# Level-four scores computed in one piece with levels 16, 32, 64 and the key transposes

## The chip, the cores and the metric

The kernel runs on one core of one Trainium2 chip. The metric is the device time of one execution in microseconds, the median over the runs of a kernel. The core has a matrix engine (PE, with its weight loads shown as PEld), a vector engine (DVE), a scalar engine (ACT), GpSimd (POOL) and a sync engine (SP) that mostly issues DMAs. Each engine works through its own queue in order and waits on semaphores for the others.

## What is computed

One layer of a decoder trunk on a sequence of 1024 tokens of width 1024, all in float32: an RMS norm modulated by a conditioning vector, one input projection, two recurrent mixers side by side, a gated merge of both, an output projection and a final norm. The two mixers are HGRN2 with 8 heads (key and value width 128) and GLA with 4 heads (key width 128, value width 256). Both run the same chunked gated linear attention; of the reference this is the part that matters here:

```python
def step(S, inp):
    qi, ki, vi, gi = inp
    b = jnp.cumsum(gi, axis=2)
    o_inter = jnp.einsum('bhck,bhkv->bhcv', qi * jnp.exp(b), S)
    diff = b[:, :, :, None, :] - b[:, :, None, :, :]
    decay = jnp.where(causal, jnp.exp(jnp.minimum(diff, 0.0)), 0.0)
    scores = jnp.einsum('bhtk,bhsk,bhtsk->bhts', qi, ki, decay)
    o_intra = jnp.einsum('bhts,bhsv->bhtv', scores, vi)
    b_last = b[:, :, -1:, :]
    S_new = S * jnp.exp(b_last[:, :, 0, :])[..., None] + jnp.einsum(
        'bhsk,bhsv->bhkv', ki * jnp.exp(b_last - b), vi)
    return S_new, o_inter + o_intra
```

## The kernel before

The projections are long matmuls: a feature block (`Feat`, L454) is 48 matmuls of 128x128 weights with 512 columns, each operand split into a rounded part and a remainder; blocks of values (`Vblk`, `Vblk2`) are built alike. They stand in a list of jobs. While a job is emitted, every unit of some six long matmuls calls `weave`, which advances a second track, `side`: the attention of one head after another, written as a generator. Each `yield n` in it asks for n units at a pace of 1.1 before the generator goes on, so the yields set how many long matmuls lie between two pieces of a head. A third track, `back`, does background work (`factors`, `weight_sums`, `gate_side`). After the jobs come the last stages (L1313), again with `weave`; the twelfth head runs there. Behind all that a planner gives each engine its final order, from what it thinks will be ready when, so a later instruction can pass an earlier one that it takes to be waiting.

`attention` works on one head, keys and queries as tiles of 128 partitions (the key channel) by 1024 tokens, in chunks of 128. The decay between two tokens is a product of per-channel gates, so scores are built from the small to the large: within groups of four tokens (matmuls L596, 32 of 80 columns), then between the four members of groups of sixteen tokens, the level of four (L628, 32 of 48 columns), then between neighbouring blocks of 16 (L683, 32 of 16 columns), of 32 (L689, 16) and of 64 tokens (L694, 8). All write the one PSUM tile `sc_ps` of two banks. Between the levels DVE multiplies the gates into the queries and keys in place (L612, L630, L633; `grow` for the levels 16, 32, 64, L656 to L659), and before each `grow` of levels 16 and 32 ACT copies the halves that the matmuls of that level need out of q and k into parts of the tile `xb` (`keep`, L648). Level 64 reads q and k themselves. Masked copies on DVE (L603 to L611 for the first level, L669 to L672 for the level of four, L698 for level 16) collect the small scores in `blk`; ACT copies (L703 to L709) put everything into `scT`. Then the keys are transposed on PE (L720, 7 transposes through PSUM tiles of the pool `ps_m`) and copied out by ACT (L721) into `kT`; state products (L742) and their accumulation (L746, L748 on DVE) and the outputs (L761, L763) follow.

The order of a head's pieces on PE, with the yields between them, is: L596, 5, L628, 7, levels 16 to 64, 3.5, transposes, 1.5, state products, 3 and so on. A set `scoring` holds a head until its scores have left `sc_ps`; the last stages ask it before they lend `sc_ps` out as an accumulator.

SBUF tiles of 4 KB per partition come from `Slots`, 46 of them, handed out first in, first out. `Stream.ahead` loads the weights of a job two jobs ahead and splits them one job ahead, if enough slots are free; `factors` and `weight_sums` wait until 12 are.

Of the kernel before, what the change touches and what calls it, by code (L numbers as in the profile page):

```python
# [15 lines left out]
P = 128  # L16
D = 1024
T = 1024
KT = D // P
NCH = T // P  # L20
# [62 lines left out]
def hybrid_trunk_kernel(  # L83
# [6 lines left out]
    nc = tc.nc  # L90
# [9 lines left out]
    S = Slots(sp, N_SLOTS)  # L100
# [7 lines left out]
    def mtile():  # L108
        cnt[0] += 1
        return ps_m.tile([P, 512], F32, tag="m", name=f"pm{cnt[0]}")  # L110

    sc_ps = ps_s.tile([P, T], F32, name="sc_ps")


    ident = cp.tile([P, P], F32, name="ident")
# [214 lines left out]
    for bi, (d0, nd) in enumerate(blocks):  # L330
        if bi:
            make_mod(d0, nd, mods.pop(bi), 0)
        for d in range(d0, d0 + nd):
# [12 lines left out]
            for f in range(NG):  # L346
                for n, (a, b) in enumerate(((0, h_hi), (1, h_hi), (0, h_lo))):
                    nc.tensor.matmul(accs[f], wg(a, d, f), b[d][:, 0:512],
                                     start=(d == 0 and n == 0), stop=(d == KT - 1 and n == 2))
# [220 lines left out]
    def attention(q, k, f, v, vo, V, post):  # L570
# [23 lines left out]
        for b in range(32):  # L594
            ch, j = b // 4, b % 4
            nc.tensor.matmul(sc_ps[32 * j:32 * j + 32, ch * P:ch * P + 80], k[:, b * 32:b * 32 + 32], xb[:, b, :],  # L596
                             start=True, stop=True)
# [27 lines left out]
        yield 5  # L625
        for b in range(32):
            ch, j = b // 4, b % 4
            nc.tensor.matmul(sc_ps[32 * j:32 * j + 32, ch * 48:ch * 48 + 48], k[:, b * 32:b * 32 + 32],  # L628
                             xf[:, b * 48:b * 48 + 48], start=True, stop=True)
# [11 lines left out]
        kept = {}  # L641
        off = [320, tot[:, 256:320]]

        def keep(n):
            at = 0 if n == 16 else 1024
            kept[n] = flat[:, at:at + 512], flat[:, at + 512:at + 1024]
            for dst, src in zip(kept[n], (pairs(k, n)[:, :, 0, :], pairs(q, n)[:, :, 1, :])):
                nc.scalar.copy(dst.rearrange("p (b n) -> p b n", n=n), src)  # L648
# [13 lines left out]
        keep(16)  # L662
# [10 lines left out]
        grow(16)  # L673
        keep(32)
        grow(32)
        yield 7


        k16, q16 = kept[16]
        k32, q32 = kept[32]  # L680
        for b in range(32):
            ch, j = b // 4, b % 4
            nc.tensor.matmul(sc_ps[32 * j:32 * j + 16, 512 + ch * 16:512 + ch * 16 + 16],  # L683
                             k16[:, b * 16:b * 16 + 16], q16[:, b * 16:b * 16 + 16], start=True, stop=True)
        for ch in range(NCH):
            for hf in range(2):
                i = 2 * ch + hf
                p0, c0 = 64 * hf + 32 * (ch % 2), ch // 2 * 32
                nc.tensor.matmul(sc_ps[p0:p0 + 32, c0:c0 + 32], k32[:, i * 32:i * 32 + 32],  # L689
                                 q32[:, i * 32:i * 32 + 32], start=True, stop=True)  # L690
        for ch in range(NCH):
            s0 = ch * P
            p0, c0 = ch % 2 * 64, 640 + ch // 2 * 64
            nc.tensor.matmul(sc_ps[p0:p0 + 64, c0:c0 + 64], k[:, s0:s0 + 64],  # L694
                             q[:, s0 + 64:s0 + 128], start=True, stop=True)
        grow(64)
        cur = off[1]
        cpr(blk[:, :, 16:32], bc(masks[16], [NCH, 16]),  # L698
            sc_ps[:, 512:640].rearrange("p (c t) -> p c t", c=NCH))
        for hf in range(2):  # L700
            for odd in range(2):
                p0 = 64 * hf + 32 * odd
                nc.scalar.copy(scT[64 * hf:64 * hf + 32, odd::2, 64 * hf + 32:64 * hf + 64],  # L703
                               sc_ps[p0:p0 + 32, 0:128].rearrange("p (c t) -> p c t", t=32))
# [6 lines left out]
        yield 3.5  # L711


        kT = S.get([NCH, P])
        for g in range(2):
            nt = 4 if g == 0 else 3
            pt = mtile()
            for i in range(nt):
                ch = g * 4 + i
                nc.tensor.transpose(pt[:, i * P:(i + 1) * P], k[:, ch * P:(ch + 1) * P], ident)  # L720
            nc.scalar.copy(kT[:, g * 4:g * 4 + nt, :].rearrange("p c s -> p (c s)"), pt[:, 0:nt * P])  # L721
        S.free(k)
        yield 1.5
# [817 lines left out]
```

## Time and profile before

| | |
|---|---|
| median of 3 runs | 1249.74 us (1246.07 to 1254.04) |
| the profiled execution | 1252.38 us, span of its profile 1250.7 us |
| mean granted clock of PE | 0.99 |
| busy: PE, PEld | 1205.7 us (96%), 999.9 us (80%) |
| busy: DVE, ACT, POOL | 765.2 us (61%), 530.4 us (42%), 132.4 us (11%) |

A row of a profile names a line of the kernel, the engine, the operation, the tiles written and read, shapes, a count and durations; where a fence is from the timeline, it begins with start and duration in us. PE's busy time counts overlapping matmuls once, and a matmul's duration reaches beyond the start of the next, so the pace of PE is read from the starts. A wait is put down to the semaphore that came last. The profiled execution is one of several, so its own time is not the median.

### The profile page before, as it was taken

What the parts mean: (1) busy time and instruction counts of PE and PEld (TensorE: products, weight loads), DVE (VectorE), ACT (ScalarE), POOL (GpSimd) and SP (SyncE); (2) the same over time, 40 slices, a digit from 0 to 9 for tenths busy, and PEclk for the clock granted to TensorE, in tenths of its full rate; (3) what the DMA queues carried; (4) which work ended last, traced back from release to release, by engine and by line L of the source; (5) the groups of instructions that cost most, each with busy time, mean ns of one, the idle gap of its engine ahead of it and who ended that gap; (6) DMA issues with size and microseconds to landing.
All of it is one profiled execution on the core that took longest, in us unless ns stands there. A gap on an engine that the chain in (4) does not pass through costs nothing.

```text
span 1250.7 us, 20782 instructions
## 1 busy us (share of the span) xinstructions
PE 1205.7 (96%) x8603; PEld 999.9 (80%) x8603; DVE 765.2 (61%) x1219; ACT 530.4 (42%) x784; POOL 132.4 (11%) x216
## 2 busy tenths in 40 slices
PE   4799999999999999999999999999999999998997
PEld 3676899989798888788887878877888888787786
DVE  5746425494857556777873365695422668979443
ACT  4467713343334344243332323456643644454222
POOL 5510000201211021021110101011110000000000
PEclk9899999999999999999999999999999999999999
DMA  8832100653644167255251212154546556235202
GB/s 269 278 115 86 52 18 18 217 188 102 203 143 144 63 208 254 92 179 174 96 177 45 60 41 68 38 183 169 173 163 225 179 171 201 83 100 170 118 34 101
DMA packets 126928, 168.82 MB, mean 135 GB/s; under 512 B 7019, under 2 KB 97185, under 8 KB 126834
## 3 DMA queue, kind: packets, MB, share of 16 engines
q1 hardware_dynamic: 115234, 129.53, 33.5%
q0 software_dynamic: 11552, 37.97, 7.8%
q8 instruction: 67, 1.10, 0.4%
q14 instruction: 27, 0.22, 0.1%
q10 hardware_dynamic: 48, 0.01, 0.0%
HBM read 125.53 MB, written 41.94 MB: 134 GB/s over the span
## 4 chain that ended last, share of the span: by engine, by line
PE 59%; issue 24%; DVE 8%; DMA 3%; POOL 2%; ACT 2%; SPq 1%; POOLq 0%; DVEq 0%; ACTq 0%
PE pd L454 13%; PE pd L1313 11%; PE sc_ps L1313 5%; PE pm L1313 5%; PE pd L556 2%; PE pd L557 2%; PE pd L558 2%; DVE scT L250 1%; PE pm L761 1%; PE pm L742 1%; PE pm L763 1%; PE pd L1083 1%; PE pd L1084 1%; PE pd L1085 1%; DVE b L195 1%
## 5 line engine op out<-in xcount | busy, mean ns | idle before, releaser
L454 PE MATMUL pd<-b,b 128*128 128x512 f32 x1632 | 386.3, 393 | 0.0
L454 PEld LDWEIGHTS pd<-b,b 128*128 128x128 f32 x1632 | 302.4, 188 | 64.0 <-issue 0.5
L1313 PE MATMUL pd<-b,b 128*128 128x512 f32 x720 | 175.7, 395 | 2.5 <-DVE b L866 1.5
L1313 PEld LDWEIGHTS pd<-b,b 128*128 128x128 f32 x720 | 134.7, 189 | 35.4 <-DVE b L866 1.9
L195 DVE TENSOR_TENSOR b<-b,b 128x1024 fp32r<-128x1024 f32 (+1 forms) x95 | 101.8, 1082 | 74.7 <-ACT b L192 34.8
L192 ACT CAST b<-b 128x1024 fp32r<-128x1024 f32 (+1 forms) x95 | 84.6, 904 | 104.0 <-DVE b L1169 14.7
L1256 DVE TENSOR_TENSOR b<-b,b 128x1024 fp32r<-128x1024 f32 x56 | 68.3, 1224 | 68.5 <-ACT b L1255 46.6
L1255 ACT CAST b<-b 128x1024 fp32r<-128x1024 f32 x56 | 58.5, 1051 | 62.8 <-PE pd L1313 17.2
L1313 PE MATMUL sc_ps<-b,b 128*128 128x512 f32 x324 | 79.0, 391 | 0.3 <-ACT scT L706 0.3
L1313 PE MATMUL pm<-b,b 128*128 128x512 f32 x300 | 72.5, 389 | 3.4 <-DVE b L1256 3.4
L513 PE MATMUL pd<-b,b 128*128 128x256 f32 x256 | 74.2, 290 | 0.0
L515 PE MATMUL pd<-b,b 128*128 128x256 f32 x256 | 72.5, 283 | 0.0
L514 PE MATMUL pd<-b,b 128*128 128x256 f32 x256 | 72.4, 283 | 0.0
L1313 PEld LDWEIGHTS sc_ps<-b,b 128*128 128x128 f32 x324 | 60.4, 188 | 13.6 <-ACT scT L706 0.8
L1313 PEld LDWEIGHTS pm<-b,b 128*128 128x128 f32 x300 | 56.3, 188 | 15.5 <-DVE b L1256 3.8
L1234 DVE TENSOR_TENSOR b<-b,b 128x1024 fp32r<-128x1024 f32 x36 | 45.1, 1263 | 18.1 <-ACT b L1233 10.3
L1171 POOL DMA_DIRECT2D ws<-b x64 | 34.6, 541 | 194.8 <-DVE b L1165 87.1
L556 PE MATMUL pd<-b,b 128*128 128x512 f32 x128 | 52.0, 406 | 0.0
L557 PE MATMUL pd<-b,b 128*128 128x512 f32 x128 | 50.4, 394 | 0.0
L558 PE MATMUL pd<-b,b 128*128 128x512 f32 x128 | 50.4, 394 | 0.0
L648 ACT COPY xb<-b 128x512 f32<-128x512 f32 x48 | 29.5, 620 | 49.3 <-PE sc_ps L628 26.3
L1233 ACT CAST b<-b 128x1024 fp32r<-128x1024 f32 x36 | 37.2, 1049 | 28.9 <-PE pd L1313 10.1
(268 smaller groups left out, 2041.9 us busy)
## 6 DMA issues: line engine op xcount, KB each, us to landing
b<-in_w_in_dram SPq DMA_DIRECT2D x66, 512.0 KB, 4.0
ws<-b POOLq DMA_DIRECT2D x64, 256.0 KB, 3.0
b<-ws SPq DMA_DIRECT2D x32, 512.0 KB, 4.2
b<-in_x_dram SPq DMA_DIRECT2D x16, 512.0 KB, 5.8
b<-in_ada_w_dram SPq DMA_DIRECT2D x32, 256.0 KB, 6.2
b<-in_w_branch_dram SPq DMA_DIRECT2D x16, 512.0 KB, 4.8
b<-h SPq DMA_DIRECT2D x14, 512.0 KB, 4.2
b<-in_w_in_dram SPq DMA_DIRECT2D x24, 256.0 KB, 3.5
```

Of the source, the lines that this page charges most:

```text
L192: i = nc.scalar.copy(hi, src)
L195: (eng or nc.vector).tensor_sub(lo, src, hi.bitcast(F32))
L454: nc.tensor.matmul(ps[0:w, th * 512:(th + 1) * 512], a[:, k, 0:w], b[:, th * 512:(th + 1) * 512], start=(k == 0 and n == 0), stop=(k == KT ...
L513: nc.tensor.matmul(o, lh, hi[:, k % 4, :], start=(k == 0), stop=False)
L514: nc.tensor.matmul(o, lh, lo[:, k % 4, :], start=False, stop=False)
L515: nc.tensor.matmul(o, ll, hi[:, k % 4, :], start=False, stop=(k == KT - 1))
L556: nc.tensor.matmul(o, lh, hi[:, k % 2, :], start=(k == 0), stop=False)
L557: nc.tensor.matmul(o, lh, lo[:, k % 2, :], start=False, stop=False)
L558: nc.tensor.matmul(o, ll, hi[:, k % 2, :], start=False, stop=(k == KT - 1))
L1255: nc.scalar.copy(hi, t)
L1256: nc.vector.tensor_sub(lo, t, hi.bitcast(F32))
L1313: nc.tensor.matmul(o, a[:, sl], c, start=(p in (1, 5) and kt == 0 and n == 0), stop=(kt == 3 and n == 2), skip_group_check=True)
```

## The change

The matmuls of the level of four are no longer issued after `yield 5`. ACT copies the keys as they stand at that level into a new tile `kc`, since DVE goes on multiplying k in place. Then all of `keep` and `grow` for 16, 32 and 64 is written at one stretch. The copies of level 16 go to the end of `xb`, which the level of four does not use; those of 32 and 64 go to two new slots. `yield 13` follows, and then one piece: the level of four, levels 16, 32 and 64, and the seven transposes. Level 64 now reads copies, because `grow(64)` has been done by then. Level 32 writes to columns 384 to 512 of `sc_ps`, so that it doesn't overwrite the level of four. The masked copies of the level of four, of level 16 and the copies into `scT` come behind the piece, then `yield 4` and the state products.

```diff
@@ -622,11 +622,8 @@
         nc.scalar.copy(X[:, :, 1:4:2, :], qg[:, :, 2:4, :])
         TT(X[:, :, 2:6:3, :], qg[:, :, 2:4, :], bc(t4[:, :, 1:3].unsqueeze(3), [64, 2, 4]), M)
         TT(X[:, :, 4, :], X[:, :, 5, :], bc(t4[:, :, 1:2], [64, 4]), M)
-        yield 5
-        for b in range(32):
-            ch, j = b // 4, b % 4
-            nc.tensor.matmul(sc_ps[32 * j:32 * j + 32, ch * 48:ch * 48 + 48], k[:, b * 32:b * 32 + 32],
-                             xf[:, b * 48:b * 48 + 48], start=True, stop=True)
+        kc = S.get([T])
+        nc.scalar.copy(kc, k)
         TT(qg[:, :, 1:4, :], X[:, :, 0:5:2, :], bc(t4[:, :, 0:1].unsqueeze(3), [64, 3, 4]), M)
         TT(t4[:, :, 2], t4[:, :, 2], t4[:, :, 3], M)
         TT(t4[:, :, 1], t4[:, :, 1], t4[:, :, 2], M)
@@ -641,9 +638,11 @@
         kept = {}
         off = [320, tot[:, 256:320]]
 
+        spare = [S.get([T]) for _ in range(2)]
+        homes = {16: flat[:, 1536:2560], 32: spare[0], 64: spare[1]}
+
         def keep(n):
-            at = 0 if n == 16 else 1024
-            kept[n] = flat[:, at:at + 512], flat[:, at + 512:at + 1024]
+            kept[n] = homes[n][:, 0:512], homes[n][:, 512:1024]
             for dst, src in zip(kept[n], (pairs(k, n)[:, :, 0, :], pairs(q, n)[:, :, 1, :])):
                 nc.scalar.copy(dst.rearrange("p (b n) -> p b n", n=n), src)
 
@@ -659,7 +658,43 @@
             TT(nxt.unsqueeze(2), left, right, M)
             off[:] = at + nb, nxt
 
-        keep(16)
+        for n in (16, 32, 64):
+            keep(n)
+            grow(n)
+        cur = off[1]
+        yield 13
+
+
+        for b in range(32):
+            ch, j = b // 4, b % 4
+            nc.tensor.matmul(sc_ps[32 * j:32 * j + 32, ch * 48:ch * 48 + 48], kc[:, b * 32:b * 32 + 32],
+                             xf[:, b * 48:b * 48 + 48], start=True, stop=True)
+        k16, q16 = kept[16]
+        k32, q32 = kept[32]
+        k64, q64 = kept[64]
+        for b in range(32):
+            ch, j = b // 4, b % 4
+            nc.tensor.matmul(sc_ps[32 * j:32 * j + 16, 512 + ch * 16:512 + ch * 16 + 16],
+                             k16[:, b * 16:b * 16 + 16], q16[:, b * 16:b * 16 + 16], start=True, stop=True)
+        for ch in range(NCH):
+            for hf in range(2):
+                i = 2 * ch + hf
+                p0, c0 = 64 * hf + 32 * (ch % 2), 384 + ch // 2 * 32
+                nc.tensor.matmul(sc_ps[p0:p0 + 32, c0:c0 + 32], k32[:, i * 32:i * 32 + 32],
+                                 q32[:, i * 32:i * 32 + 32], start=True, stop=True)
+        for ch in range(NCH):
+            p0, c0 = ch % 2 * 64, 640 + ch // 2 * 64
+            nc.tensor.matmul(sc_ps[p0:p0 + 64, c0:c0 + 64], k64[:, ch * 64:ch * 64 + 64],
+                             q64[:, ch * 64:ch * 64 + 64], start=True, stop=True)
+        kT = S.get([NCH, P])
+        for g in range(2):
+            nt = 4 if g == 0 else 3
+            pt = mtile()
+            for i in range(nt):
+                ch = g * 4 + i
+                nc.tensor.transpose(pt[:, i * P:(i + 1) * P], k[:, ch * P:(ch + 1) * P], ident)
+            nc.scalar.copy(kT[:, g * 4:g * 4 + nt, :].rearrange("p c s -> p (c s)"), pt[:, 0:nt * P])
+        S.free(k, kc, *spare)
         px = sc_ps[:, 0:384].rearrange("p (g s n) -> p g s n", s=6, n=4)
         bv = blk.rearrange("p c t -> p (c t)").rearrange("p (g r n) -> p g r n", r=4, n=4)
         for g in range(2):
@@ -670,57 +705,20 @@
             cpr(bg[:, :, 2:4, :], bc(mg[:, :, 1:4:2, :], [NCH, 2, 4]), pg[:, :, 1:4:2, :])
             cpr(bg[:, :, 2:4, :], bc(mg[:, :, 2:6:3, :], [NCH, 2, 4]), pg[:, :, 2:6:3, :])
             cpr(bg[:, :, 3, :], bc(mg[:, :, 4, :], [NCH, 4]), pg[:, :, 4, :])
-        grow(16)
-        keep(32)
-        grow(32)
-        yield 7
-
-
-        k16, q16 = kept[16]
-        k32, q32 = kept[32]
-        for b in range(32):
-            ch, j = b // 4, b % 4
-            nc.tensor.matmul(sc_ps[32 * j:32 * j + 16, 512 + ch * 16:512 + ch * 16 + 16],
-                             k16[:, b * 16:b * 16 + 16], q16[:, b * 16:b * 16 + 16], start=True, stop=True)
-        for ch in range(NCH):
-            for hf in range(2):
-                i = 2 * ch + hf
-                p0, c0 = 64 * hf + 32 * (ch % 2), ch // 2 * 32
-                nc.tensor.matmul(sc_ps[p0:p0 + 32, c0:c0 + 32], k32[:, i * 32:i * 32 + 32],
-                                 q32[:, i * 32:i * 32 + 32], start=True, stop=True)
-        for ch in range(NCH):
-            s0 = ch * P
-            p0, c0 = ch % 2 * 64, 640 + ch // 2 * 64
-            nc.tensor.matmul(sc_ps[p0:p0 + 64, c0:c0 + 64], k[:, s0:s0 + 64],
-                             q[:, s0 + 64:s0 + 128], start=True, stop=True)
-        grow(64)
-        cur = off[1]
         cpr(blk[:, :, 16:32], bc(masks[16], [NCH, 16]),
             sc_ps[:, 512:640].rearrange("p (c t) -> p c t", c=NCH))
         for hf in range(2):
             for odd in range(2):
                 p0 = 64 * hf + 32 * odd
                 nc.scalar.copy(scT[64 * hf:64 * hf + 32, odd::2, 64 * hf + 32:64 * hf + 64],
-                               sc_ps[p0:p0 + 32, 0:128].rearrange("p (c t) -> p c t", t=32))
+                               sc_ps[p0:p0 + 32, 384:512].rearrange("p (c t) -> p c t", t=32))
         for odd in range(2):
             nc.scalar.copy(scT[0:64, odd::2, 64:128],
                            sc_ps[64 * odd:64 * odd + 64, 640:896].rearrange("p (c t) -> p c t", t=64))
         for j in range(4):
             nc.scalar.copy(scT[32 * j:32 * j + 32, :, 32 * j:32 * j + 32], blk[32 * j:32 * j + 32])
         scoring.discard(me)
-        yield 3.5
-
-
-        kT = S.get([NCH, P])
-        for g in range(2):
-            nt = 4 if g == 0 else 3
-            pt = mtile()
-            for i in range(nt):
-                ch = g * 4 + i
-                nc.tensor.transpose(pt[:, i * P:(i + 1) * P], k[:, ch * P:(ch + 1) * P], ident)
-            nc.scalar.copy(kT[:, g * 4:g * 4 + nt, :].rearrange("p c s -> p (c s)"), pt[:, 0:nt * P])
-        S.free(k)
-        yield 1.5
+        yield 4
         per = 512 // V
         spp = 1024 // V
         st = [S.get([1024]) for _ in range((7 + spp - 1) // spp)]
```

## The prediction

> **What bounds the kernel now.** I read the page's busy shares first, then the busy time of the stretch that holds the heads, then the waits of PE, and last the timeline of single heads.
>
> ```profile
> span 1250.7 us, 20782 instructions
> PE 1205.7 (96%) x8603; PEld 999.9 (80%) x8603; DVE 765.2 (61%) x1219; ACT 530.4 (42%) x784; POOL 132.4 (11%) x216
> 180.00:830.00 650.00, 644.26 (x5895) 546.93 (x5893) 422.60 (x762) 248.75 (x377) 80.89 (x112) 1.00 0.40 128
> ```
>
> The last row is the stretch in which eleven of the twelve heads run woven into the projections (columns: length, then PE, PEld, DVE, ACT, POOL busy, clock, DMA share, GB/s). PE is busy 644.3 of 650 us at full clock; DVE has 35% to spare, ACT 62%. So a thing counts here only if it shortens PE's own queue or one of PE's few waits. The longest waits of PE between 175 and 875 us (total, times, longest) are:
>
> ```profile
> PE sc_ps L596 <- DVE xb L592: 1.8, 2, 0.9
> PE sc_ps L628 <- DVE tot L631: 1.4, 1, 1.4
> PE sc_ps L683 <- DVE blk L672: 1.4, 1, 1.4
> PE pm L742 <- ACT b L721: 0.7, 2, 0.4
> PE sc_ps L628 <- DVE blk L611: 0.2, 1, 0.2
> ```
>
> The change touches the last four of these, 3.7 us in all. L628 is the level of four, L683 the first of levels 16, 32, 64, L742 the state products behind the transposes.
>
> **What joining saves on PE.** No matmul goes or comes: 32 + 32 + 16 + 8 matmuls and 7 transposes per head stay. What goes is the entry and exit of a piece among the long matmuls. Head 6 in the timeline of PE (start, duration, count; the third row is the same piece cut at 521.85, the last the group of all L628: busy, mean ns, idle before):
>
> ```profile
> 520.19 1.07 PE L454 MATMUL pd<-b,b 128*128 128x512 f32 x4
> 521.19 0.89 PE L628 MATMUL sc_ps<-xb,b 128*32 128x48 f32 x64
> 521.65 0.43 PE L628 MATMUL sc_ps<-xb,b 128*32 128x48 f32 x23
> 522.01 8.45 PE L454 MATMUL pd<-b,b 128*128 128x512 f32 x36
> 530.39 0.67 PE L683 MATMUL sc_ps<-xb 128*16 128x16 f32 x62
> L628 PE MATMUL sc_ps<-xb,b 128*32 128x48 f32 x768 | 10.7, 207 | 1.7 <-DVE tot L631 1.4 <-DVE blk L611 0.2
> ```
>
> Thirty-six long matmuls take 530.39 - 522.01 = 8.38 us, 0.23 each. The four ahead of L628 take 1.00: three of 0.23 and 0.31 for the last, so the entry costs 0.31 - 0.23 = 0.08 to 0.09. The 23 last starts of L628 lie 0.010 apart (0.43 less one duration of 0.207, over 22), so the last one starts at 521.87 and the next long one 0.14 later: the exit costs 0.13. Together 0.215 us per piece; a joined level of four pays neither, since level 16 works with the same narrow outputs in column groups and follows at the same pace. 12 x 0.215 = 2.6 us.
>
> The transposes bring nothing. Head 5:
>
> ```profile
> 478.56 0.67 PE L683 MATMUL sc_ps<-xb 128*16 128x16 f32 x62
> 480.11 0.73 PE L454 MATMUL pd<-b,b 128*128 128x512 f32 x2
> 483.87 0.62 PE L454 MATMUL pd<-b,b 128*128 128x512 f32 x2
> 484.33 0.93 PE L720 MATMUL pm<-ident,b 128*128 128x128 f32 x7
> 485.01 0.47 PE L454 MATMUL pd<-b,b 128*128 128x512 f32 x1
> ```
>
> L720 enters at the long matmuls' own step (483.87, 484.10, 484.33) and leaves at once: its 0.68 us are work, and the exit behind L694, at the end of levels 16 to 64 (480.11 - 478.56 = 1.55 us with it), stays, in front of a transpose. Taken at zero; bounds one exit as L628's, 12 x 0.13 = 1.6 us, either way.
>
> **What it adds on ACT.** Per head one copy of k, 128x1024, and two copies of level 64, 128x512; prices are those of L588 and L648.
>
> ```profile
> L588 ACT COPY xb<-b 128x1024 f32<-128x1024 f32 x12 | 12.6, 1049 | 22.9 <-PE sc_ps L689 14.5 <-DVE b L866 7.9 <-DVE b L294 0.6
> L648 ACT COPY xb<-b 128x512 f32<-128x512 f32 x48 | 29.5, 620 | 49.3 <-PE sc_ps L628 26.3 <-DVE b L633 19.3 <-DVE b L657 2.1
> L657 DVE TENSOR_TENSOR b<-b,tot 128x512 f32<-128x512 f32 x36 | 24.6, 684 | 2.3 <-ACT xb L648 2.3
> ```
>
> 1.05 + 2 x 0.62 = 2.29 us, 27.5 us over twelve heads, in an engine that idles some 400 us of that stretch. Cost zero while PE's work covers it; without that cover, all 27.5. Queued behind it on ACT are evacuations of the projections and casts of weights; those are prepared a whole job (11 us) ahead. No DMA is added or moved.
>
> **The wait that replaces two.** Now the level of four needs only kc and xb, which are there early, but PE's next matmuls in the piece need the copies and multiplications of all three levels, and the transposes need the last `grow`. The joined piece stands 13 units behind L596; L683 stood 5 + 7 = 12 behind, with a piece of 0.82 us between. A unit is six long matmuls over the pace 1.1, 1.37/1.1 = 1.25 us, so PE comes to the piece 1.25 - 0.82 = 0.4 us later than it came to L683, if nobody waits. The chain it waits for, in head 6 on DVE and ACT, then a group of masked copies over all heads, then DVE's other work in head 2 between 256.6 and 266.3 (busy, mean ns):
>
> ```profile
> 518.43 1.03 DVE L630 TENSOR_TENSOR b<-xb,tot 128x768 f32<-128x768 f32 x1
> 522.15 0.96 DVE L633 TENSOR_TENSOR b<-b,tot 128x768 f32<-128x768 f32 x1
> 526.84 0.68 DVE L656 TENSOR_TENSOR b<-b,tot 128x512 f32<-128x512 f32 x1
> ...
> 518.58 1.03 ACT L865 ACTIVATE b<-pd 128x1024 f32<-128x1024 f32 x1 [3.37 <-PE pd L454]
> 522.84 1.05 ACT L192 CAST b<-b 128x1024 fp32r<-128x1024 f32 x1 [3.23 <-DMA b<-in_w_in_dram]
> ...
> L670 DVE COPY_PREDICATED blk<-mask,sc_ps 128x64 f32<-128x64 int32 x24 | 5.4, 225 | 0.0
> L672 DVE COPY_PREDICATED blk<-mask,sc_ps 128x32 f32<-128x32 int32 x24 | 4.5, 187 | 0.0
> ...
> L1136 DVE TENSOR_TENSOR b<-b,b 128x1024 f32<-128x1024 f32 x4 | 4.9, 1222 | 0.4 <-DMA b<-h 0.4
> L195 DVE TENSOR_TENSOR b<-b,b 128x1024 fp32r<-128x1024 f32 x1 | 1.3, 1252 | 0.0
> ```
>
> L633 today waits until L628 has read k; with kc it may follow L630 (end 519.46) as soon as the copy is made. From L633's start to the end of level 32 are 527.52 - 522.15 = 5.4 us, of which 1.1 is one cast of weights that ACT put in between; level 64 adds one more round of copies and multiplications, at least 2 x 0.68 = 1.4, at most 1.24 + 1.37 = 2.6. The sum is 5.7 to 8.0; PE gives 530.8 - 519.5 = 11.3 us. The masked copies that stood in this chain, twice these two rows (L671 and L669 are like them), 19.8/12 = 1.65 us a head, move behind the piece. So head 6 has 3 us of slack or more, and the heads like it.
>
> Head 2 has not. There DVE does 4.9 + 1.3 us of other work in those 9.7 us, on top of 0.96 + 6 x 0.68 + some 1 us of small ones: 12.2 of 9.7, though the small ones run in ACT's shadows. I take 1.5 us for it, like its present wait of 1.4, and 0.5 for the other heads together. Bounds for the new wait: 0, and 1.5 in each of twelve heads, 18; I take 2.0, nearer the first, because only one wait of this kind stands in today's rows.
>
> **What stands behind the piece.** `yield 4` follows (5 us) before the state products, where 1.5 (1.9 us) stood between transposes and L742: the copies of kT get 3 us more, and L742's 0.7 goes. The copies into scT and the masked ones now have 4 + 3 units, 8.7 us, until L761. The first and the last of these copies on ACT in head 6:
>
> ```profile
> 534.83 1.06 ACT L703 COPY scT<-sc_ps 32x128 f32<-32x128 f32 x4 [0.37 <-DVE blk L698]
> 538.22 0.97 ACT L721 COPY b<-pm 128x512 f32<-128x512 f32 x2
> ```
>
> All twelve, the two of kT with them, take 539.19 - 534.83 = 4.4 us; the masked copies add 1.65 on DVE, 6.0 together. Cost zero; if DVE is 3 us behind, a wait of about 1 us comes back at L761, which lies in the range.
>
> **Slots.** Three more of 46 are held from behind L596 to the end of the piece. By the code's own bookkeeping the leanest heads (2 and 4) have five or six free there, so two remain; the one large preparation in such a stretch, of a value block of 512 columns, needs nine and finds twelve today. Loads and preparations stay where they are. The background work that asks for twelve free slots (`factors`, `weight_sums`) is put off in heads 1 to 4, and its results are needed only hundreds of us later. Zero.
>
> **The sum.** -2.6 (entries and exits) - 1.6 (L628) - 1.4 (L683) - 0.7 (L742) + 2.0 (new wait) = -4.3 us. On the profiled execution, 1252.38 us with its span of 1250.7 and 1.7 around it, that gives 1248.1. That execution lies 2.6 above the median of the three runs, 1249.74; on the median the same sum gives 1245.4 us.
>
> [...] The clock in two adjoining stretches behind the matmuls of the gate at 657 us, where PE is busy throughout but half of its matmuls use one row:
>
> ```profile
> 658.00:661.40 3.40, 3.40 (x8) 0.88 (x6) 0.00 (x0) 2.03 (x3) 0.00 (x0) 1.00 0.00 0
> 661.40:664.80 3.40, 3.40 (x8) 2.48 (x8) 1.23 (x1) 0.85 (x2) 0.00 (x0) 0.50 0.10 20
> ```
>
> A thin stretch of 3.4 us was followed by 3.4 us at half clock, a loss of 1.7. The joined piece is 0.69 + 1.55 + 0.68 = 2.9 us of short matmuls and transposes; today the longest piece of scores is 1.55. [...]
>
> **The rivals.**
> - *The waits come back.* The joined piece, L742 or L761 together wait as long as PE does now, and 2.6 us more: saved and paid alike, 1249.7 us. For it: head 2's DVE is full in any order. Against: the order of DVE's work no longer hangs on L628.
> - *The chain is late in every head* (slower). PE comes to the piece before the last `grow` has ended; from the point at which other DVE and ACT work in those 11 us passes about 4 us, each head pays. At head 2's 1.5 us in twelve heads: -2.6 - 3.7 + 18 = +11.7, 1261.4 us. For it: the extra ACT copies stand inside the chain, kc ahead of L633. Against: ACT idled 3.4 and 3.2 us in head 6's rows.
> - *The clock drops behind each piece* (slower): if the piece counts as thin like the gate's stretch, each head loses 1.7 us, -4.3 + 12 x 1.7 = +16.1, 1265.8 us. Against: level four and 64 use all 128 rows and column groups side by side, and no head shows it.
> - *More is gained*: DVE's order becomes so even that L596 and the rest of PE's waits go too, and no new wait comes, -2.6 - 1.8 - 3.7 = -8.1, 1241.6 us. To pass 1% it would have to reach beyond the heads.
> - *The piece is not joined*: PE's order is planned, and if the planner thinks level 16 late, it puts long matmuls between, as it split levels 16 to 64 of head 12 today:
>
> ```profile
> 843.72 0.63 PE L683 MATMUL sc_ps<-xb 128*16 128x16 f32 x56
> 844.47 3.01 PE L1313 MATMUL pd<-b,b 128*128 128x512 f32 x12
> ```
>
> Then the 2.6 is not saved: 1248.0 us.
>
> **How the numbers follow.** Forecast 0.45, waits back 0.14, not joined 0.11, more gained 0.14, chain late 0.13, clock 0.03. A measurement tells about 1% (12.5 us) from no change. Beyond that on the fast side (under 1237.2) lies a third of the cases with more gained, 0.05; on the slow side (over 1262.2) the clock and half of the late chains, 0.10; within it 0.85. The range leaves out the clock, the dearer half of the late chains and the far end of more gained: 1238 to 1258. The likeliest case alone, with the new wait between 0 and 6, spans 1243 to 1250.
>
> **What would show it.** In the changed profile one group of 64 level-four matmuls runs straight into level 16, with no long matmul between, and the transposes follow level 64 directly; waits on the level of four and on the state products are gone; the waits of the first level-16 matmul and of the transposes on DVE or ACT tell the new term, 2 us here; ACT is busy 27 us longer, DVE as long as before. PEclk stays 1.00 between 180 and 830 us. The prediction is wrong if PE's idle time there rises above 6 us, or if the span moves by more than the heads' stretch does.

## The result and the profile after

The changed kernel takes 1267.18 us (median of 6 runs, 1265.49 to 1270.72) against 1250.00 us before (6 runs): ratio 1.0145, interval 1.0124 to 1.0165. The forecast was 1245.4 us with a range up to 1258; it missed by 21.8 us, on the wrong side. The profiled execution took 1267.32 us.

The head of the page after, and then the busy time of the stretch from 180 to 830 us (columns as in the prediction):

```profile
span 1265.4 us, 20847 instructions
PE 1207.2 (95%) x8603; PEld 1004.9 (79%) x8603; DVE 766.8 (61%) x1219; ACT 555.9 (44%) x820; POOL 132.4 (10%) x216
```

```profile
180.00:830.00 650.00, 633.42 (x5797) 541.48 (x5796) 414.03 (x749) 263.94 (x400) 79.44 (x111) 0.99 0.39 124
```

Over the whole execution ACT is busy 25.5 us longer, near the 27 forecast, and DVE 1.6. But PE idles 16.6 us in that stretch, where it idled 5.7. The prediction named 6 us as the mark above which it is wrong. The waits of PE between 175 and 875 us (total, times, longest):

```profile
PE sc_ps L596 <- DVE xb L592: 4.5, 3, 3.8
PE pd L1311 <- ACT b L1285: 3.5, 1, 3.5
PE pm L759 <- DVE b L746: 3.5, 4, 1.5
PE pm L759 <- ACT scT L719: 2.3, 2, 1.8
PE sc_ps L687 <- issue: 2.1, 1, 2.1
PE sc_ps L683 <- issue: 1.8, 1, 1.8
PE sc_ps L687 <- ACT xb L588: 1.6, 1, 1.6
PE sc_ps L1311 <- ACT scT L716: 1.0, 1, 1.0
PE pm L695 <- issue: 0.5, 1, 0.5
PE pd L1311 <- ACT b L1381: 0.4, 1, 0.4
PE pm L740 <- DVE b L746: 0.3, 1, 0.3
```

In the new numbering L670, L677, L683 and L687 are the level of four, 16, 32 and 64, L695 the transposes, L740 the state products, L759 the outputs, L1311 the last stages. The three waits that were to go are gone: nothing waits on the level of four or on `blk` in front of level 16, and 0.3 us is left at L740. In their place stand four things, 21.2 us together: the first level of a head (4.5), stops inside the joined piece (2.1 + 1.8 + 1.6 + 0.5 = 6.0), the outputs (5.8), and the last stages behind head 12 (4.9).

**Where the time went.** The same long matmul, the first of the feature blocks behind a value block, on PE of before and of after, behind the first level of head 5, when the first four heads are through their scores:

```profile
463.83 1.07 PE L454 MATMUL pd<-b,b 128*128 128x512 f32 x4
```

```profile
460.81 1.07 PE L454 MATMUL pd<-b,b 128*128 128x512 f32 x4
```

Here the changed kernel is 3.0 us ahead; at head 1's first level it was 0.25 us behind. So far it looks like the forecast, but only a part of the gain is shown to come from joining. From the first level of head 1 to that of head 5 PE takes 280.87 us before and 277.59 after. The kernel before with three slots withheld and nothing joined (below) takes 278.35 there, and 279.08 and 279.46 in its two other forms, of which the last has the code of the kernel before in heads 1 to 4. The waits in front of the level of four and of level 16 thus shrink in kernels that join nothing, and by over 1 us from one execution to the next. What joining saves shows in head 1, where PE waits for nothing: 68.28 us to the first level of head 2, against 68.65 before and 68.60 with the piece broken in two. That is 0.37 us a head, where 0.215 was forecast.

The same comparison at the next value block (631.78 and 635.62 us) shows it 3.8 behind, at the start of the last stages (825.71 and 835.39) 9.7, and behind head 12 16. The losses lie in heads 6 to 12.

**The stops in the piece.** Head 6 on PE:

```profile
533.62 0.89 PE L670 MATMUL sc_ps<-xb,b 128*32 128x48 f32 x64
534.32 0.71 PE L677 MATMUL sc_ps<-xb 128*16 128x16 f32 x62
...
535.32 0.27 PE L687 MATMUL sc_ps<-b 128*64 128x64 f32 x1
537.72 0.68 PE L687 MATMUL sc_ps<-b 128*64 128x64 f32 x15 [2.14 <-issue]
538.34 0.98 PE L695 MATMUL pm<-ident,b 128*128 128x128 f32 x7
```

PE runs from the level of four straight into level 16, so the piece is joined. Then it stops for 2.14 us between the first and the second matmul of one line; "issue" means that nothing in the profile releases it. The three others of this kind are alike (the one put down to L588 as well: that copy fills `xb` for the next head, which level 64 does not read, and it had ended 0.8 us before PE went on). What moves at that moment is seen in the DMA queues. The profile names queue q8 one of instructions; its row for the window 535.20 to 535.35 us, and then the one for 691.70 to 691.90 us, ahead of the stop in head 9, from which PE comes back at 694.25:

```profile
q8 instruction: 1, 0.02, 48.9%
...
q8 instruction: 1, 0.02, 32.7%
```

From 533.5 to 535.2 and from 535.35 to 537.7 us there is no such packet. So the transfer of one block of instructions begins at about 535.3 us, and PE goes on 2.45 us later; in heads 4, 8 and 9 it is 2.35 to 2.45. The page of before counts the blocks:

```profile
q8 instruction: 67, 1.10, 0.4%
```

1.10 MB in 67 packets are 16.4 KB each, and 17,206 matmuls and weight loads over 67 are 257 instructions a block. A long matmul and its load take 0.23 us, so a block of them lasts some 29 us. The joined piece has 183 matmul rows and as many loads in 2.9 us: 256 of these rows last some 2.0 us, less than the 2.35 to 2.45 us from the start of a packet to PE's next matmul.

The trace shows the blocks directly. Number the rows of PE and PEld from 0 in the order of their starts, those of the sequencer with them. The matmul behind each stop then has a number that leaves 193 or 194 when divided by 256. That holds for the four stops here and for all thirty in the runs below, and for none of the other 201 waits of PE over 0.2 us between 175 and 1000 us in the eighteen kernels. So these stops lie whole multiples of 256 rows apart, give or take one row, the size of a block: PE stops at the edge of a block. It also matters where in the piece the edge lies: the four stops stand 304 to 364 rows into the piece, while the edges in the other heads lie at 287 rows or fewer, or behind the end of the piece, and stop nothing. With levels doubled side by side the stops stand at 254 rows or more. A piece of 224 rows doesn't reach so far; the one stop in a run of that length, below, stands at 73 rows, two units behind another such run. Why that one came is open. The prediction did not weigh the supply of instructions.

**The first level of head 6.** PE, then DVE ahead of it, then SP between 455 and 520 us:

```profile
513.22 2.36 PE L596 MATMUL sc_ps<-xb,b 128*32 128x80 f32 x64 [3.80 <-DVE xb L592]
```

```profile
505.03 0.69 DVE L1164 TENSOR_TENSOR b<-b,b 128x512 f32<-128x512 f32 x1 [1.02 <-DMA b<-in_w_in_dram]
...
507.69 0.81 DVE L989 TENSOR_SCALAR b<-b,oml,lb 128x1024 f32<-128x1024 f32 x1
...
512.43 0.64 DVE L592 TENSOR_TENSOR xb<-xb,b 128x256 f32<-128x256 f32 x1
```

```profile
SPq L1157 <- DMA yh<-b: 6.6, 1, 6.6
```

Read from below: a load of `weight_sums` (L1157) on SP waits 6.6 us until the store of an earlier head's output (`yh`) has read its slot. The load lands at 505 us; the four additions of `weight_sums` (L1163 to L1167) stand in DVE's queue ahead of L989, which prepares head 6. What L989 reads comes from ACT. Before, these are the row of ACT and the row of DVE that reads it, and after, the row of ACT for L989 above:

```profile
505.27 1.03 ACT L989 ACTIVATE b<-pd 128x1024 f32<-128x1024 f32 x1 [8.04 <-PE pd L454]
506.33 0.81 DVE L991 TENSOR_SCALAR b<-b,oml,lb 128x1024 f32<-128x1024 f32 x1 [0.74 <-ACT b L989]
```

```profile
502.66 1.03 ACT L987 ACTIVATE b<-pd 128x1024 f32<-128x1024 f32 x1
```

Before, DVE starts as soon as ACT has ended, at 506.3 us. After, ACT ends at 503.7 and DVE starts at 507.7, 4.0 us later. That makes L592 late, and PE waits 3.8 us for it. Before, no wait of SP on a store of `yh` stands in this window, and head 6 waited 0.9 us. Behind this wait, and behind the one of 3.5 us in the last stages, the clock is halved, from 512.1 to 518.9 us and from 846.6 to 850.0. Two windows from there:

```profile
512.80:516.20 3.40, 2.98 (x66) 2.69 (x67) 3.26 (x6) 0.93 (x2) 0.00 (x0) 0.50 0.25 87
...
846.40:849.80 3.40, 3.40 (x10) 2.58 (x10) 3.10 (x4) 0.18 (x1) 0.00 (x0) 0.52 0.00 0
```

**Head 12 in the last stages.** ACT:

```profile
841.81 1.05 ACT L1231 CAST b<-b 128x1024 fp32r<-128x1024 f32 x1 [3.76 <-DMA b<-fx]
...
844.54 1.04 ACT L626 COPY b<-b 128x1024 f32<-128x1024 f32 x1
845.48 0.58 ACT L1285 ACTIVATE b<-pd 128x512 f32<-128x512 f32 x1
```

L1285 empties the accumulator for which PE waits 3.5 us. Ahead of it in ACT's queue stand casts that were late for their DMA, and the new copy of k (L626).

### The profile page after: what moved, and what is told of

Same layout as the page of the kernel before. It is cut to its first block, busy times and chain, and to the rows that moved or that the text cites. A ratio compares the mean times of both kernels' runs of the same rounds, so it can differ in the third digit from the quotient of the medians.

```text
span 1265.4 us, 20847 instructions
## 1 busy us (share of the span) xinstructions
PE 1207.2 (95%) x8603; PEld 1004.9 (79%) x8603; DVE 766.8 (61%) x1219; ACT 555.9 (44%) x820; POOL 132.4 (10%) x216
## 5 line engine op out<-in xcount | busy, mean ns | idle before, releaser
L1311 PE MATMUL pd<-b,b 128*128 128x512 f32 x720 | 177.0, 397 | 4.4 <-ACT b L1285 3.5
L1311 PEld LDWEIGHTS pd<-b,b 128*128 128x128 f32 x720 | 135.9, 191 | 36.9 <-ACT b L1285 4.5
L1253 ACT CAST b<-b 128x1024 fp32r<-128x1024 f32 x56 | 58.5, 1051 | 58.0 <-PE pd L1311 17.2
L1311 PE MATMUL sc_ps<-b,b 128*128 128x512 f32 x324 | 78.8, 391 | 1.0 <-ACT scT L716 1.0
L1311 PE MATMUL pm<-b,b 128*128 128x512 f32 x300 | 72.6, 390 | 3.4 <-DVE b L1254 3.4
L1311 PEld LDWEIGHTS sc_ps<-b,b 128*128 128x128 f32 x324 | 60.5, 188 | 14.3 <-ACT scT L716 1.4
L1311 PEld LDWEIGHTS pm<-b,b 128*128 128x128 f32 x300 | 56.2, 188 | 15.5 <-DVE b L1254 3.8
L759 PE MATMUL pm<-scT,b 128*128 128x128 f32 x256 | 47.5, 277 | 5.8 <-DVE b L746 3.5
```

The source lines that it names most:

```text
L1253: nc.scalar.copy(hi, t)
L1311: nc.tensor.matmul(o, a[:, sl], c, start=(p in (1, 5) and kt == 0 and n == 0), stop=(kt == 3 and n == 2), skip_group_check=True)
```

## The experiments

All ratios are against the kernel before, run on the same chip beside it.

**The run broken.** Two units of long matmuls behind the level of four:

```diff
-        yield 13
+        yield 11
 (level of four)
+        yield 2
 (levels 16, 32, 64, transposes)
```

> The changed kernel with a break of two units (some 11 long matmuls) between the level of four and level 16; yields 11, 2, 4 in place of 13, 4. Theory A (the joined piece takes PE's instructions faster than they are fetched: three pieces stood still inside with no wait on another engine, and one more with a late releaser, 6.3 us together): those stops vanish, less than 0.6 us of them is left, and some 3 us of the gain go through to the time after 2.6 us for the entries and exits are paid again: 1263 to 1265 us. Rival (the stops are waits on ACT or DVE that the profile does not name, since level 64 and the transposes wait for the last multiplications): they stay, 4 us or more, and the time is 1267 to 1270.

Measured 1254.90 us, ratio 1.0054 (1.0039 to 1.0069). No stop without a releaser is left. Its longest waits:

```profile
PE sc_ps L596 <- DVE xb L592: 4.4, 2, 3.9
PE pd L1310 <- ACT b L1284: 2.8, 1, 2.8
PE pm L758 <- DVE b L745: 2.8, 4, 0.8
```

The change lost 17.2 us against its kernel before, this form 6.1, so breaking the run gives back 11. Of that 6.0 are the stops themselves; the rest went with them (outputs 5.8 to 2.8, last stages 4.9 to 3.3, and half clock for 3.4 us in place of 10.2), which is why the expectation, 1263 to 1265, was too high. That the stops caused this rest is argued from their going together. The other 6 us of the loss stay, with the wait of head 6.

**The run lengthened.** The changed kernel with the level of four twice:

```diff
+        for b in range(32):
+            nc.tensor.matmul(sc_ps[...], kc[...], xf[...], ...)
         for b in range(32):
             nc.tensor.matmul(sc_ps[...], kc[...], xf[...], ...)
```

> The changed kernel with the 32 matmuls of the level of four issued twice, one set behind the other, at the head of the joined piece: 64 matmuls and 64 weight loads more in each run of short instructions. The work alone is 0.69 us a head, 8.3 us in all: 1267.2 + 8.3 = 1275.5 us. Theory (PE runs through its short instructions faster than they are fetched): the run is now some 490 instructions in 3.6 us, so the stops without a releaser come in most of the twelve heads, 1 to 2.4 us each, 12 to 25 us in place of 6.3: 1281 to 1294 us. Rival (the four stops come from something else at those moments and not from the length of the run): the same four stops, 1275.5 us.

Measured 1287.94 us, ratio 1.0292 (1.0259 to 1.0325), inside the theory's range. Stops of the piece, 175 to 1000 us:

```profile
PE sc_ps L685 <- issue: 10.4, 4, 3.4
PE sc_ps L689 <- issue: 5.6, 3, 2.0
...
PE sc_ps L685 <- ACT xb L588: 2.5, 1, 2.5
```

With three smaller ones they are 21.8 us in eleven places, in place of 6.0 in four. The packets tell whose instructions q8 carries: the program has 1,536 matmuls and loads more, and q8 73 packets in place of 67, 256 for each.

**The run alone, in the kernel before.** Levels 16 to 64 issued twice, side by side or with two units between (then `yield 1.5` in place of 3.5 ahead of the transposes):

```diff
         (levels 16, 32, 64)
+        yield 2        # only in the second of the two runs
+        (levels 16, 32, 64 once more)
```

> The kernel before with the matmuls of levels 16, 32 and 64 issued twice, one set right behind the other: 1.55 - 0.13 = 1.42 us of work more in each head, 17.0 us in all, and runs of some 450 short instructions in place of 224. No slot, copy or multiplication differs from the kernel before. Theory (short instructions are used up faster than they are fetched): stops without a releaser in most heads, 10 to 20 us, 1276 to 1286 us. Rival (stops need the other parts of the change): 1266 us.

> The same matmuls twice, but with two units of long matmuls between the two sets, so that no run is longer than in the kernel before (224 instructions): 12 x (1.55 + 0.08) = 19.6 us of work. Theory: no stops without a releaser, 1268 to 1269 us, less than with the sets side by side though the work is more. Rival (extra instructions cost fetches wherever they stand): the same stops as with the sets side by side, 1276 us or more.

Measured 1295.81 us (1.0377, 1.0359 to 1.0396) side by side and 1292.95 us (1.0348, 1.0330 to 1.0367) apart. The stops of the first, then the two rows of the second that matter:

```profile
PE sc_ps L698 <- issue: 13.9, 7, 3.8
PE sc_ps L709 <- issue: 4.9, 3, 2.5
...
PE sc_ps L704 <- issue: 1.3, 1, 1.3
```

```profile
PE pm L758 <- ACT b L737: 8.1, 12, 0.9
...
PE sc_ps L699 <- issue: 1.2, 1, 1.2
```

Eleven stops, 20.1 us, against one of 1.2: no slot, copy or order of the change is needed for them, only the length of the run. The clock adds to the first: behind five of its stops, 1.7 to 3.8 us long, it is halved for 3.4 us or 6.8 (from 200.1, 275.2, 353.7, 428.8 and 794.0 us), 20.4 us in all and some 9 us lost, which is why it too came out slower than expected. In the second no stop has half clock behind it. But it missed its expectation by 24 us for reasons of its own: with the transposes closer, the state products wait 8.1 us in twelve heads for the copies of kT, the gate came behind a wait of 2.3 us and ran at half clock for 10.2 us, and the second set cost 2.05 us in head 1, where 1.63 was reckoned. The times of the two don't tell the theories apart; the rows do.

**The slots alone.** The kernel before with three slots withheld behind the first level until the end of levels 16 to 64; and the copies and slots of the change with PE's pieces where they were:

```diff
+        held = [S.free_list.popleft() for _ in range(3)]
 ...
         grow(64)
+        S.free_list.extend(held)
```

> The kernel before, but three slots are taken out of the list behind the first level and put back at the end of levels 16 to 64; nothing is written to them and no instruction of a head is added. Theory B (slots: the background work moves, blocks DVE's queue ahead of a later head's first level, and that costs the wait of 3.8 us and the 1.7 us of half clock of head 6): a wait of 2 us or more at the first level of a middle head and 1253 to 1258 us. Rival (slots do not matter, the order of PE's pieces does): 1248 to 1252 us, PE's waits as in the kernel before.

> The changed kernel's copies and early multiplications with all of PE's pieces where they stood before: yields 5, 7, 3.5, 1.5. The 27 us of ACT copies and the three slots stay. If the joining alone costs the time (theories A and C): no stops inside the pieces, waits at the outputs below 2 us, the 3.0 us of waits at the level of four and level 16 gone, 1246 to 1250 us. If copies and slots cost it (theory B, or ACT's load): 1255 us or more.

Measured 1256.31 us (1.0058, 1.0040 to 1.0076) and 1258.19 us (1.0072, 1.0055 to 1.0090). Head 6 waits 3.3 and 2.7 us at its first level, without any stop in a piece. So the slots, priced at zero, cost 7.5 us without a joined piece, and 9.4 with the copies and their order.

**How the slots cost.** The first idea was that they put off the background work, which asks for twelve free ones. The loads of the second half of `weight_sums` in before and after (duration, first and last start):

```profile
L1159 SPq DMA_DIRECT2D b<-in_w_branch_dram x16: 367/368/465, 451.6 to 574.3; - x16
```

```profile
L1157 SPq DMA_DIRECT2D b<-in_w_branch_dram x16: 367/368/812, 490.9 to 706.5; - x16
```

They are put off by 39 to 132 us. Three runs let it start at nine free slots, in the changed kernel, in the broken form and in the kernel before with three slots withheld:

```diff
-            while len(S.free_list) < 12:
+            while len(S.free_list) < 9:
```

> The changed kernel, in which the background work (factors and weight_sums) asks for nine free slots in place of twelve. That puts its pieces back among the heads where they stood before the change, or somewhat earlier. Theory (the three slots put the background off, and its waits for DMAs then hold DVE ahead of the first level): the wait of 3.8 us at the first level of head 6 and the half clock behind it go, about 7 us; the stops inside the joined piece stay: 1260 us. Rival (DVE is late at head 6 because of the changed order inside the heads): 1267 us.

> The joined piece broken by two units of long matmuls behind the level of four (1254.9 us when measured with twelve slots), and the background work asks for nine free slots. If the two causes are separate, their parts add: 1254.9 - 7 = 1248 us, as fast as before the change or a little faster. Rival (with the break the background's shift no longer costs anything): 1255 us.

> The kernel before with three slots withheld from behind the first level to the end of levels 16 to 64 (1256.3 us when measured), and the background work asks for nine free slots in place of twelve, so that it is not put off. Theory (withholding slots costs only because the background is put off): 1249 to 1250 us, the wait at the first level under 2 us again. Rival (withheld slots delay loads or preparations of the projections): 1256 us.

Measured 1262.77 us (1.0106, 1.0072 to 1.0140), 1260.84 us (1.0081, 1.0053 to 1.0110) and 1266.02 us (1.0123, 1.0089 to 1.0157): a little better than the change, 6 us worse than the broken form, 10 worse than the withheld slots alone. The wait of head 6 stayed, 3.7, 3.4 and 2.2 us. The theory failed here. Nine is also earlier than before, so two runs, the broken form and the withheld slots, wrote each background piece at its old place:

```diff
-            while len(S.free_list) < 12:
+            for _ in range(pins.popleft()):   # 34, 0, 11, 0, 0, 1, 0, 0, 15, 0 ...
                 yield 1
```

> The joined piece broken by two units (1254.9 us when measured), and the background work doesn't ask for free slots at all: each of its pieces waits for as many units as it waited for in the kernel before (34, 0, 11, 0, 0, 1, 0, 0, 15, then 0), so that it is written at the very places where it was before the change. Theory (the three slots cost by putting the background off): the wait of 3.9 us at the first level of head 6 and the collision with the gate at 795 us go, 1247 to 1250 us. Rival (three slots fewer in circulation make each load wait for a later reader, wherever it is written): head 6 still waits over 3 us, 1254 to 1256 us.

> The kernel before with three slots withheld in each head (1256.3 us when measured), and the background work written at the very places where it stands in the kernel before. Nothing else differs from the kernel before. Theory (the put-off background costs): 1249 to 1250 us. Rival (nearer reuse of the slots costs, with the background in its place too): the first level of head 6 waits 3 us as before the pinning, 1254 to 1257 us.

Measured 1255.67 us (1.0052, 1.0035 to 1.0070) and 1266.48 us (1.0139, 1.0118 to 1.0159). The second is the kernel before but for the three slots, with the background where it was, and it is as slow as the change. Its longest waits:

```profile
PE sc_ps L684 <- DVE blk L673: 4.9, 2, 3.5
PE pm L744 <- ACT b L723: 4.0, 3, 2.5
PE sc_ps L596 <- DVE xb L592: 2.9, 1, 2.9
```

So the putting off is not the main thing. The last pair withheld the slots in some heads only:

```diff
-        held = [S.free_list.popleft() for _ in range(3)]
+        held = [S.free_list.popleft() for _ in range(3 if me <= 4 else 0)]   # or 0 if me <= 4 else 3
```

> The kernel before with three slots withheld in heads 1 to 4 only (1256.3 us when withheld in all twelve). The background work is put off there by the demand for twelve free slots, and meets heads 7 to 9; the last eight heads have all their slots. If what costs is that the background is put off: 1254 to 1257 us. If what costs is the smaller supply of slots in the later heads: 1249 to 1250 us, and the first level of head 6 waits under 1 us.

> The complement: three slots withheld in heads 5 to 12 only, so that the background stands where it does in the kernel before until head 5. If the putting off costs: 1249 to 1250 us. If the smaller supply costs in the heads themselves (loads wait for later readers of their slot, and DVE behind them): 1255 to 1257 us, with 3 us of waiting at the first level of head 6.

Measured 1252.83 us (1.0024, 1.0010 to 1.0038) and 1263.26 us (1.0110, 1.0095 to 1.0125). Neither time lies in a range expected. The supply in the later heads costs most, 14.7 us; withholding in the first four, which puts the background off, costs 4.3. In the second, SP and the first level of head 6:

```profile
SPq L1161 <- DMA yh<-b: 5.6, 1, 5.6
```

```profile
PE sc_ps L596 <- DVE xb L592: 3.3, 2, 2.9
```

The wait of SP on a store of `yh`, between 455 and 520 us, is there in each of the thirteen kernels that hold the slots in head 5 and later, with the background at its old places or not (4.1 to 6.6 us), and each has 2.2 to 3.9 us of waiting in head 6. It is in none of the five others (before, the two with levels doubled, slots in the first four heads only, and the last run below), and these wait 0.9. So the two go together in all eighteen kernels, and the rows above show the steps between; no run takes away the one wait of SP alone. How the whole cost of the slots, 4 to 17 us over these arrangements, splits over the other waits stays open; the costs don't add, since both halves withheld together cost 7.5. Nor does a run hand the slots out in another order without withholding any, so fewer slots and another order of slots aren't told apart.

**The outputs.** The piece two units earlier, so that the copies behind it have six units in place of four:

```diff
-        yield 13
+        yield 11
 ...
-        yield 4
+        yield 6
```

> The changed kernel with yields 11 and 6 in place of 13 and 4: the joined piece two units earlier, the state products where they were. Theory C (the masked copies and the copies into the score tile come too late for the output products, 6.5 us of waits at the outputs): these waits fall below 2 us, and the time to 1261 to 1264 us, unless the earlier piece waits for the multiplications, at most 2 us. Rival (the waits at the outputs come from DVE's other work): they stay above 4 us and the time at 1266 to 1269.

Measured 1265.65 us, ratio 1.0139 (1.0110 to 1.0167).

```profile
PE sc_ps L685 <- issue: 7.0, 3, 3.7
PE sc_ps L596 <- DVE xb L592: 5.8, 3, 3.2
...
PE pm L757 <- ACT scT L717: 1.8, 1, 1.8
```

The wait of the outputs falls from 5.8 to 1.8 us, so it does come from too few units. But the stops grew from 6.0 to 7.3 and head 6 waits as before; the time hardly moves. The expectation, 1261 to 1264 us, was too low.

**Only some heads changed.** The broken form with pinned background, for heads 1 to 11, and for heads 1 to 4:

```diff
+        if me < 12:        # or: if me <= 4
             (broken form)
+        else:
+            (order of the kernel before)
```

> As the run with break and pinned background, but the twelfth head, in the last stages, has the order of the kernel before (its pieces 5, 7, 3.5 and 1.5 units apart, no extra copies or slots). Theory (the copies that joining adds delay ACT's work for the last stages there, 3.5 us of waiting and as much again at half clock and behind): about 5 us less than with all twelve heads changed. Rival (the last stages wait for something that the head's order doesn't move): the same time.

> The broken form of the joined piece in the first four heads (those of GLA) alone; the eight others have the order of the kernel before; the background work is written where it stands in the kernel before. Theory (in the first four heads the change gains what was forecast, 3 to 4 us, and what is lost is lost later): 1245 to 1246 us, faster than both kernels. Rival (the gain there is given back wherever PE next waits for DVE or a DMA): 1249 us.

Measured 1254.17 us (1.0035, 1.0021 to 1.0048) and 1248.92 us (0.9998, 0.9984 to 1.0012), each of 10 runs. With head 12 as it was, 1.5 us come back, not 5, and the intervals overlap: the wait of 3.3 us on L1286 goes and one of 2.3 us on DVE takes its place. With the GLA heads alone changed, the kernel is as fast as before, not 3 to 4 us faster. Its longest waits are those of before, less the ones on the level of four and on level 16:

```profile
PE sc_ps L596 <- DVE xb L592: 1.8, 2, 0.9
PE pd L1413 <- DVE b L964: 1.5, 1, 1.5
```

Its profiled execution is 2.1 us better off between 187 and 464 us, which is within what single executions of a kernel differ by (1246.84 to 1251.80 for the kernel before). No version here beats the kernel before.

## Why the prediction was wrong

- In *What joining saves on PE* the saving was priced too low, not too high: joining saves 0.37 us in head 1, where 0.215 was forecast; an exit in front of the transposes, taken at zero and bounded by 0.13, would make up most of the difference. *What it adds on ACT* held, 25.5 us. The waits at L628, L683 and L742 are gone, but the first two shrink as well in kernels that join nothing, so that the gain of 3.3 us at 464 us can't be credited to the joining as a whole.
- The step that failed first is that *What joining saves on PE* priced a run only by its entry and exit. The missing term is the supply of instructions: a run of 366 in 2.9 us, where the longest before had 224 in 1.55. It costs 6.0 us of stops, and 11 with what went with them when the run was broken.
- *The wait that replaces two* was forecast at 2.0 us, for copies and multiplications ahead of levels 16 to 64 and the transposes. No wait on them stands in the rows; what the piece waits for is its own instructions.
- *Slots* said zero, the second step that failed. It counted free slots and asked whether a preparation would find enough. Slots go round first in, first out, so with three fewer a load gets a slot that was freed later, waits on SP for its last reader, and holds up DVE's queue behind it; the rows show this for head 6. Withheld alone, the slots cost 7.5 us, and 4 to 17 in other arrangements.
- *What stands behind the piece* was sized at zero, with 1 us in the range; it measured 5.8. Two units more bring it to 1.8, the break to 2.8. That DVE was 3 us behind, the condition named there, was not measured.
- The clock rival, 1265.8 us, lies nearest to the measured time, by luck. It was right in what it watched, but no piece of the changed kernel has half clock behind it; two waits of over 3 us do, for 6.8 and 3.4 us, some 4.5 us lost. In the two runs with longer pieces it comes behind eight of 22 stops, 1.7 to 3.8 us long, and not behind others as long; what decides it stays open.
- The late chain, the slower rival at 1261.4 us, was nearer in size than the forecast too, but its mechanism did not come.

## What to carry to other kernels

Count the matmuls and loads in a run of short ones. Here runs of 366 in 2.9 us stopped PE for 6.0 us in four heads, and with two units of long matmuls inside, the longest run 238, no such stop was left and the kernel was 11 us better off. A buffer taken from a shared pool is never free because enough are left (three of 46 withheld cost 7.5 us here): ask which reader each later load then waits for, and who stands behind that load. In this kernel, with PE 96% busy, two waits of 3.8 and 3.5 us cost more than the three of 1.6, 1.4 and 0.7 us that were removed.

## What was not expected of the hardware

PE went on 2.35 to 2.45 us after the transfer of an instruction block of 16.4 KB, some 256 PE instructions, had begun, and 2.2 to 2.9 us after it in the runs with doubled levels; inside runs of about 450 short instructions it stopped for up to 3.8 us. These stops have no releaser in the profile, or one that the matmul does not depend on; counting the rows by 256 tells them from every other wait. Runs of up to 224 showed none in the kernel before and one of 1.2 us in twelve heads with doubled levels, and runs of 238 none in the broken form. Behind eight of the 22 stops in the two runs with longer pieces, 1.7 to 3.8 us long, came 3.4 us or more at half clock.
